# The sample's rows in the value products of heads 2 to 4: eight fp32 products on four column parts of the array

## The chip, the cores and the metric

The kernel runs on one core of one Trainium2 chip. The metric is the device time of one execution in microseconds (us), lower is better. Engines are named as in the profile: PE is TensorE (matrix products), PEld its weight load, DVE is VectorE, ACT is ScalarE, POOL is GpSimd, and SP is SyncE, whose queue issues nearly all DMAs here.

## What is computed

Two layers of a streaming encoder, for a prompt of 1024 tokens and, beside it, a sample of 32 tokens of another sequence with a carried state. Layer 0 mixes with an mLSTM (a matrix memory per head, four heads), layer 1 with attention in a band; each is followed by an MLP with squared ReLU. All is fp32. The part that matters here is the input of layer 0's mixer:

```python
def mlstm_mixer(u, ...):
    proj = u @ w_in                                   # u: tokens x 1024
    qk_pre = proj[..., :2 * QK_A]                     # 4 heads x 128, twice
    v = proj[..., 2 * QK_A:2 * QK_A + V_A]            # 4 heads x 256
    ...
    q, k = silu(causal_conv(qk_pre))                  # per head 128 wide
    # per chunk of tokens, per head: a matrix memory C (256 x 128)
    num = (q k^T * weights) v + a * (C q);  C = a_last * C + (w_s v)^T k
```

For each head, v is the product of all 1056 tokens (1024 of the prompt, then 32 of the sample) with 256 columns of `w_in`.

## The kernel before

**Number format of the products.** In the trace an fp32r product of 256 columns takes 0.12 us of PE, an fp32 product of 257 columns 0.44 us. To keep fp32 accuracy at the cheaper pace the kernel splits each operand into a high and a low fp32r part: ACT copies the raw value into the high part (L89) and DVE subtracts to get the low part (L90). A product is then three matmuls: high x high, high x low, low x high. `U` holds the modulated tokens already split (two parts, 8 chunks of 128 rows, 1056 tokens), and `wtile` loads 512 rows of a weight into a `raw` tile and splits it into a `w` tile.

**The value product.** `v_weight(h, half)` (L473) loads and splits one half (512 rows) of the 256 columns of head h. `v_chunk` (L483) does the three matmuls of one token tile and one chunk of rows; the tokens are the stationary operand (128 of them), the weights move (256 columns). There are NT = 9 token tiles: eight of the prompt and, as the ninth, the sample's 32 tokens, for which 128 columns of `U` are taken too (behind the last token lie 96 zero columns). A tile thus has 24 matmuls. `v_out` (L491) copies the result with ACT into a `vt` tile (tag "vt", nine buffers) and POOL writes 1.0 into two further columns.

`v_first` does head 1 (h = 0 in the code), three tiles at a time, with a chunk of each in turn, since its first tiles are produced only then; its eight extra columns are the gates. `v_proj` (L501) does heads 2 to 4 (h = 1 to 3), one tile after the other.

**The order of the work.** Per head h = 1 to 3 the program says `qk_proj(h)`, then `v_proj(h)`, then starts the recurrence `mlstm(h)`. `qk_proj` has 2 x 3 groups of 24 matmuls, then per half a convolution on DVE (L608 and L611, four passes) and a SiLU in three pieces of 353 columns (L613 to L618), each with a temporary of tag "tmp" (three buffers of 384 columns). The recurrence of head h - 1 is a generator: `flow.tick` lets it take one step (one chunk of 128 tokens) after each group or tile, so that its scores (L668, L669), sums (L686, L688) and updates (L690) come between the products of head h. Chunk 8, the last, is the sample; its start state comes in a `raw` tile (`cl`).

Outside the parts marked `manual_schedule` a planner sets the order on each engine and on each DMA queue from its own costs and from what waits for what. Buffers are shared by tag: PSUM tiles of tag "mm" (three buffers) serve the `qk`, `v` and `o` products; `raw` tiles (three buffers, of which one holds a sum of the conditioning, `ada_acc`, through this phase) serve all weights.

In the same phase the conditioning (`ada`) of the later parts is computed on DVE (L279 and the lines after it), a few operations per tick. `ada_mm` (L432) is the conditioning's first product, done at the start: fp32, with 32 stationary columns, on four column parts of the array side by side.

Of the kernel before, what the change touches and what calls it, by code (L numbers as in the profile page):

```python
# [8 lines left out]
F32 = mybir.dt.float32  # L9
F32R = mybir.dt.float32r  # L10
# [5 lines left out]
P = 128  # L16
D = 1024
KC = D // P
TP = 1024
TS = 32  # L20
T = TP + TS
NT = T // P + 1
# [53 lines left out]
def trunk_kernel(ctx: ExitStack, tc: tile.TileContext, a, o):  # L76
    nc = tc.nc
    flow = Flow()
    cp = ctx.enter_context(tc.tile_pool(name="const", bufs=1, reuse_waits="tile"))
# [4 lines left out]
    def raw_tile(shape, name):  # L84
        return ring.tile(shape, F32, tag="raw", name=name, bufs=3)

    def split(dst_h, dst_l, src, eng=None):

        nc.scalar.copy(dst_h, src)  # L89
        (eng or nc.vector).tensor_sub(dst_l, src, dst_h.bitcast(F32))  # L90

    def wtile(name, srcs, ncols=256, pool=None, eng=None, between=None):

        raw = raw_tile([P, 4, ncols], f"raw_{name}")
        for dst, src in srcs(raw):
            nc.sync.dma_start(dst, src)
        if pool is None:
            w = ring.tile([P, 2, 4, ncols], F32R, tag="wc", name=f"w_{name}", bufs=6)
        else:
            w = pool.tile([P, 2, 4, ncols], F32R, tag="h", name=f"w_{name}", bufs=5)  # L100
        if between:
            between()
        split(w[:, 0], w[:, 1], raw, eng)
        return w

    def wblock(name, src, r0, c0, eng=None):

        return wtile(name, lambda raw: [(raw, src[r0:r0 + 512, c0:c0 + 256].rearrange("(k p) c -> p k c", p=P))],
                     eng=eng)
# [19 lines left out]
    nc.vector.tensor_add(sel, ident[:, 0:32], ident[:, 32:64])  # L129
    for i in (64, 96):  # L130
        nc.vector.tensor_add(sel, sel, ident[:, i:i + 32])
    ones_d = cp.tile([P, P], F32R, name="ones_d")
    nc.vector.memset(ones_d.bitcast(F32), 1.0 / D)
    eps_ln = cp.tile([P, 1], F32, name="eps_ln")
    nc.vector.memset(eps_ln, LN_EPS)
    eps_hn = cp.tile([P, 1], F32, name="eps_hn")
# [36 lines left out]
    def mmt(name):  # L173
        return pa.tile([P, 512], F32, tag="mm", name=name, bufs=3)
# [191 lines left out]
    up_cm = tc.tile_pool(name="upool", bufs=1, side="right", reuse_waits="tile")  # L366
    upool = up_cm.__enter__()
    UF = KC * T
    U = upool.tile([P, 2 * UF + 96], F32R, name="U")
    nc.vector.memset(U[:, 2 * UF:].bitcast(F32), 0.0)  # L370

    def uap(hl, k, t0, n):
        off = hl * UF + k * T + t0
        return U[:, off:off + n]

# [11 lines left out]
    A = A_cm.__enter__()  # L387
# [82 lines left out]
    G = None  # L470
    cst = {}

    def v_weight(h, half):  # L473
        def srcs(raw):
            r0 = 512 * half
            r = [(raw[:, :, 0:256],
                  w_in[r0:r0 + 512, 1024 + h * 256:1024 + (h + 1) * 256].rearrange("(k p) c -> p k c", p=P))]
            if h == 0:
                r.append((raw[:, :, 256:264], w_in[r0:r0 + 512, 3072:3080].rearrange("(k p) c -> p k c", p=P)))
            return r  # L480
        return wtile(f"v{h}_{half}", srcs, 264 if h == 0 else 256)

    def v_chunk(ps, ws, t, k):  # L483
        w = ws[k // 4]
        n = w.shape[-1]
        uh, ul = uap(0, k, t * P, P), uap(1, k, t * P, P)
        nc.tensor.matmul(ps[:, :n], uh, w[:, 0, k % 4, :], start=(k == 0), stop=False)
        nc.tensor.matmul(ps[:, :n], uh, w[:, 1, k % 4, :], start=False, stop=False)
        nc.tensor.matmul(ps[:, :n], ul, w[:, 0, k % 4, :], start=False, stop=(k == KC - 1))

    def v_out(ps, h, t):  # L491
        m = P if t < NT - 1 else TS
        vt = A.tile([P, 258], F32, tag="vt", name=f"vt_{h}_{t}", bufs=9)
        nc.scalar.copy(vt[:m, :256], ps[:m, :256])
        nc.gpsimd.memset(vt[:m, 256:258], 1.0)
        if h == 0:
            nc.vector.tensor_copy(bass.AP(g64.tensor, g64[:m, t, 0:4].offset, [g64[:m].ap[0], [32, 2], [1, 4]]),
                                  ps[:m, 256:264].rearrange("p (a b) -> p a b", a=2))
        return vt

    def v_proj(h, after):  # L501
        ws = [v_weight(h, half) for half in range(2)]
        vts = []
        for t in range(NT):
            ps = mmt(f"v_{h}_{t}")
            for k in range(KC):
                v_chunk(ps, ws, t, k)
            vts.append(v_out(ps, h, t))
            after(t)
        return vts  # L510

    def v_first(ws, nxt):


        vts = []
        for bi, (t0, n) in enumerate(TBS):
            ts = range(t0 // P, (t0 + n + P - 1) // P)
            pss = {t: (mmt, nmt, mmt)[bi % 2 * (t % 2)](f"v_0_{t}") for t in ts}
            for k in range(KC):
                for t in ts:  # L520
                    v_chunk(pss[t], ws, t, k)
                nxt(bi, k)
            vts += [v_out(pss[t], 0, t) for t in ts]
        return vts
# [58 lines left out]
    def qk_proj(h, after):  # L583
        def srcs(r0):
            return lambda raw: [(raw[:, :, j * P:(j + 1) * P],
                                 w_in[r0:r0 + 512, j * 512 + h * P:j * 512 + (h + 1) * P].rearrange(
                                     "(k p) c -> p k c", p=P)) for j in range(2)]
        ws = [wtile(f"qk{h}_{i}", srcs(512 * i)) for i in range(2)]
        out = []
        for j in range(2):  # L590
# [181 lines left out]
    for k in range(2):  # L772
        ada_mm(k)
    vw = [v_weight(0, 0)]
    adaw += [ada_load(k) for k in (6, 7)]
    for k in range(2, 4):
# [5 lines left out]
    for k in range(6, 8):  # L782
        ada_mm(k)
    vw.append(v_weight(0, 1))
    x_load(*TBS[1])
    x_load(*TBS[2], wc_tile)
# [15 lines left out]
    vts = [v_first(vw, next_u)]  # L802
# [23 lines left out]
    for h in range(1, NH):  # L826
        unit = [0]

        def after_qk():
            unit[0] += 1  # L830
            if h > 1 or unit[0] >= 3:
                flow.tick()
        if h == 1:
            ml = flow.add(mlstm(0, *qk[0], vts[0]))
        qk.append(qk_proj(h, after_qk))
        vts.append(v_proj(h, tick))
        flow.finish(ml)
        ml = flow.add(mlstm(h, *qk[h], vts[h]))
# [35 lines left out]

    T_cm = tc.tile_pool(name="temps", bufs=1, reuse_waits="tile")
    T_ = T_cm.__enter__()

    def tmp_t(shape, name, dt=F32):
        return T_.tile(shape, dt, tag="t", name=name, bufs=5)

# [18 lines left out]
    def acc_dma(d, x, out=False):  # L899
        for i in range(0, KC, 4):  # L900
            p = [d[:, i:i + 4], x[:, i:i + 4]]
            nc.sync.dma_start(*(p if out else reversed(p)))
# [681 lines left out]
    mm, norm, _, out_proj, _, add_gated_at = make_layer(acc, bank, uap)  # L1584
# [38 lines left out]
    class L0:  # L1623
# [13 lines left out]
        def rows(k, n, hl):  # L1637
            return U[:, hl * UF + k * T:hl * UF + (k + n) * T].rearrange("p (k t) -> p k t", t=T)

# [30 lines left out]
        def after(blk):  # L1670
            t0, n = blk
            ti = TBS.index(blk)
            flow.finish(norms["ada"])
            norms[ti] = flow.add(norm(ti, 1, f"n01_{ti}", W01[ti], False, lambda ti: acc_dma(
                xsp[1][:, :, t0:t0 + n], acc[ti], True)), now=NOW)
# [11 lines left out]
    for gi, grp in enumerate(((0, 1, 2), (3,))):  # L1687
        ws = {pr: [wblock(f"q{pr}_{half}", wq, 512 * half, 256 * pr) for half in range(2)] for pr in grp}
        for ti, (t0, n) in enumerate(TBS):
# [9 lines left out]
            for fc in [f for pr in grp for f in (2 * pr, 2 * pr + 1)]:  # L1699
                g, r = fc // 2, 2 * (fc % 2)  # L1700
                gp, e = g // 2, g % 2
                ps = mm(f"q_{fc}_{t0}")
# [238 lines left out]
    for t in range(NT):  # L1941
# [4 lines left out]
        m = P if t < NT - 1 else TS  # L1946
# [220 lines left out]
```

## Time and profile before

| | |
|---|---|
| median of 3 runs | 2409.55 us (2406.93 to 2409.78) |
| profiled execution | 2412.41 us, span 2410.6 us |
| PE busy | 2342.7 us (97%), 17180 matmuls |
| PEld | 2250.4 us (93%) |
| DVE | 1939.0 us (80%) |
| ACT | 1206.0 us (50%) |
| POOL | 168.1 us (7%) |
| mean granted clock of TensorE | 0.995 |
| value products of heads 2 to 4 | first starts at 127.2 us, last at 307.2 us |

The span is the profiled part of an execution, and the time includes what lies around it. A matmul's busy time overlaps that of its neighbours, because matmuls are pipelined; the time that one takes from PE is the distance between two starts. In rows of instructions in order of time the columns are the start, the duration, engine, line, operation, the output and inputs, the part of the array (128*32 is 128 rows by 32 columns), the shape, and the count of instructions merged; in brackets stands the idle time ahead of it and what ended that. The phase of layer 0's mixer, in which the change lies, ends near 440 us.

### The profile page before, as it was taken

Reading aid. Unit: us, or ns where it says so; the run is one execution under the profiler, and the core shown is the slowest. Engines: PE = TensorE matmul, PEld = TensorE weight load, DVE = VectorE, ACT = ScalarE, POOL = GpSimd, SP = SyncE. Lnnn points to the kernel's source line nnn. Section 1 sums busy time; section 2 is a strip of 40 time slices with the busy share of each in tenths; the row PEclk is TensorE's granted clock in tenths of the full one; section 3 lists DMA queues with packets and bytes.
Section 4 is the critical chain, followed back from the end, with each engine's and each line's share of the span. In section 5 each row is a group of like instructions: output and inputs, shape, how many; then the busy total and the mean of one; then the engine's idle time right before and its main releaser. Section 6 shows DMA issues by size and latency. Waiting matters only on the chain. (4 is left out here: it accounts for less than half of the span.)

```text
span 2410.6 us, 44188 instructions
## 1 busy us (share of the span) xinstructions
PE 2342.7 (97%) x17180; PEld 2250.4 (93%) x17180; DVE 1939.0 (80%) x3903; ACT 1206.0 (50%) x2454; POOL 168.1 (7%) x320
## 2 busy tenths in 40 slices
PE   7999999999999999999999999999999999899997
PEld 4999999999999999999999987789999999899997
DVE  4888766778788789989888777756998889888778
ACT  4565557278666630101147467773776777222212
POOL 0111100000000000000000224420000000000003
PEclk9999999999999999999999999999999999999999
DMA  8343222526566896675512330051486779976642
GB/s 302 120 131 103 78 89 66 177 91 206 184 198 200 279 336 230 252 261 215 183 56 89 82 93 1 10 140 59 165 278 211 259 278 335 355 256 236 224 146 73
DMA packets 284277, 424.64 MB, mean 176 GB/s; under 512 B 15384, under 2 KB 205228, under 8 KB 278948
## 3 DMA queue, kind: packets, MB, share of 16 engines
q1 hardware_dynamic: 279860, 391.48, 48.3%
q10 hardware_dynamic: 4208, 30.35, 3.1%
q8 instruction: 135, 2.21, 0.4%
q14 instruction: 74, 0.61, 0.1%
HBM read 305.96 MB, written 118.17 MB: 176 GB/s over the span
## 5 line engine op out<-in xcount | busy, mean ns | idle before, releaser
L1082 DVE SCALAR_TENSOR_TENSOR ACX<-dn,ada,ACX 128x264 f32<-128x264 f32 (+6 forms) x664 | 281.8, 447 | 83.2 <-PE dn L1452 41.1
L1452 PE MATMUL dn<-fx,wf_d 128*128 128x264 f32 x2016 | 254.1, 285 | 6.8 <-DVE ACX L1082 3.5
L1452 PEld LDWEIGHTS dn<-fx,wf_d 128*128 128x128 f32 x2016 | 248.8, 188 | 9.0 <-DVE ACX L1082 3.0
L89 ACT CAST w_dn<-raw_dn 128x1024 fp32r<-128x1024 f32 x36 | 37.7, 1050 | 282.1 <-DVE aw L279 136.9
L118 PE MATMUL dn<-hs,w_dn 128*128 128x384 f32 (+2 forms) x512 | 161.2, 315 | 0.0
L119 PE MATMUL dn<-hs,w_dn 128*128 128x384 f32 (+2 forms) x512 | 161.0, 315 | 0.0
L120 PE MATMUL dn<-hs,w_dn 128*128 128x384 f32 (+2 forms) x512 | 156.4, 314 | 1.3 <-DVE w_dn L90 1.3
L1317 PE MATMUL up<-TF,wf_u 128*128 128x264 f32 x1056 | 143.2, 285 | 3.8 <-ACT H L1320 3.8
L1317 PE MATMUL up<-U,wf_u 128*128 128x264 f32 x1056 | 140.3, 285 | 1.7 <-ACT H L1320 1.2
L1317 PE MATMUL up<-u,wf_u 128*128 128x264 f32 x1056 | 139.7, 285 | 1.3 <-ACT wf_u L89 0.7
L279 DVE SCALAR_TENSOR_TENSOR aw<-radw,cs,aw 128x512 f32<-128x512 f32 x196 | 139.5, 743 | 1.1 <-DMA radw<-in_w_ada_dram 1.1
L1317 PEld LDWEIGHTS up<-TF,wf_u 128*128 128x128 f32 x1056 | 134.4, 189 | 4.8 <-ACT H L1320 4.6
L1317 PEld LDWEIGHTS up<-U,wf_u 128*128 128x128 f32 x1056 | 133.0, 188 | 3.0 <-ACT H L1320 1.6
L1317 PEld LDWEIGHTS up<-u,wf_u 128*128 128x128 f32 x1056 | 132.9, 188 | 1.9 <-ACT wf_u L89 0.9
L118 PE MATMUL dn<-U,w_dn 128*128 128x384 f32 (+2 forms) x416 | 129.4, 312 | 0.6 <-DVE ada L304 0.6
L119 PE MATMUL dn<-U,w_dn 128*128 128x384 f32 (+2 forms) x416 | 129.4, 312 | 0.0
L120 PE MATMUL dn<-U,w_dn 128*128 128x384 f32 (+2 forms) x416 | 125.9, 313 | 0.6 <-DVE w_dn L90 0.5
L1817 ACT ACTIVATE p<-p,mx 128x576 f32<-128x576 f32 (+9 forms) x132 | 86.6, 657 | 27.5 <-DVE mx L1814 25.2
L120 PEld LDWEIGHTS dn<-hs,w_dn 128*128 128x128 f32 x512 | 96.0, 188 | 2.0 <-DVE w_dn L90 1.8
L118 PEld LDWEIGHTS dn<-hs,w_dn 128*128 128x128 f32 x512 | 96.5, 189 | 0.1
L119 PEld LDWEIGHTS dn<-hs,w_dn 128*128 128x128 f32 x512 | 96.6, 189 | 0.0
L90 DVE TENSOR_TENSOR HL<-H,HL 128x1056 fp32r<-128x1056 f32 x64 | 80.3, 1254 | 20.0 <-ACT HL L89 19.9
(403 smaller groups left out, 7111.0 us busy)
## 6 DMA issues: line engine op xcount, KB each, us to landing
hpl<-HL SPq DMA_DIRECT2D x144, 264.0 KB
rdn_u<-in_w_up_dram SPq DMA_DIRECT2D x64, 512.0 KB
hd<-HL SPq DMA_DIRECT2D x28, 1056.0 KB
fx<-hd SPq DMA_DIRECT2D x50, 528.0 KB
radw<-in_w_ada_dram SPq DMA_DIRECT2D x24, 1024.0 KB
hd<-HM SPq DMA_DIRECT2D x28, 792.0 KB
raw_up<-in_w_up_dram SPq DMA_DIRECT2D x40, 512.0 KB
raw_dn<-in_w_down_dram SPq DMA_DIRECT2D x36, 512.0 KB
```

Source lines behind the costliest of these rows:

```text
L89: nc.scalar.copy(dst_h, src)
L90: (eng or nc.vector).tensor_sub(dst_l, src, dst_h.bitcast(F32))
L118: nc.tensor.matmul(ps, wh, mov(0, k), start=(k == 0), stop=False)
L119: nc.tensor.matmul(ps, wh, mov(1, k), start=False, stop=False)
L120: nc.tensor.matmul(ps, wl, mov(0, k), start=False, stop=(k == nk - 1))
L279: nc.vector.scalar_tensor_tensor(acc[cnd], raw[:, k], sc, acc[cnd], op0=ALU.mult, op1=ALU.add)
L1082: nc.vector.scalar_tensor_tensor(xs, ps[:, off + o:off + o + mm_], gate[:, fc, cnd:cnd + 1], xs, op0=ALU.mult, op1=ALU.add)
L1317: nc.tensor.matmul(p, self.ws[w][:, wl, k], moving(f, tp, xl, k), start=first and k + n_ == 0, stop=k == 3 and n_ == 2, skip_group_check=n ...
L1452: nc.tensor.matmul(p, ws[w][:, wl, k], t[:, s0, xl], start=first and k + n_ == 0, stop=k == kg - 1 and n_ == 2, skip_group_check=not first)
L1817: nc.scalar.activation(z, z, AF.Exp, bias=mx[:, 0:1], scale=-1.0, accum_out=mx[:, 1:2])
```

## The change

For heads 2 to 4 the sample leaves the row of tiles. `v_proj` now first adds the two parts of the sample's tokens back into plain fp32 (`us`, 128 x 8 x 32, in a buffer of tag "tmp"). While each half of the weight is loaded, and ahead of its split, `v_sample` multiplies four chunks of `us` with the raw fp32 weight, chunk k on column part k of the array, into the partitions 32k to 32k + 31 of one PSUM tile of tag "mm"; the second half adds to the first. `v_out` copies the first 32 partitions and adds the three others on DVE. Then one tick follows, and then the eight tiles of the prompt.

The sample's `vt` tile moves to a tag of its own ("vs", two buffers), and "vt" has eight buffers instead of nine. In head 1 the sample's tile now has 32 stationary columns instead of 128, so the 96 zero columns of `U` and their memset go. `ones_d`, a constant for the norms, moves from the pool of constants to the pool of temporaries that opens after this phase.

```diff
-            between()
+            between(raw)
         split(w[:, 0], w[:, 1], raw, eng)
...
-    ones_d = cp.tile([P, P], F32R, name="ones_d")
-    nc.vector.memset(ones_d.bitcast(F32), 1.0 / D)
...
-    U = upool.tile([P, 2 * UF + 96], F32R, name="U")
-    nc.vector.memset(U[:, 2 * UF:].bitcast(F32), 0.0)
+    U = upool.tile([P, 2 * UF], F32R, name="U")
...
-    def v_weight(h, half):
+    def v_weight(h, half, between=None):
...
-        return wtile(f"v{h}_{half}", srcs, 264 if h == 0 else 256)
+        return wtile(f"v{h}_{half}", srcs, 264 if h == 0 else 256, between=between)
...
     def v_chunk(ps, ws, t, k):
-        uh, ul = uap(0, k, t * P, P), uap(1, k, t * P, P)
+        m = P if t < NT - 1 else TS
+        uh, ul = uap(0, k, t * P, m), uap(1, k, t * P, m)
+        ps = ps[:m]
...
+    def v_sample(us, ps, half, raw):
+
+        for k in range(4):
+            nc.tensor.matmul(ps[32 * k:32 * k + 32, :256], us[:, 4 * half + k], raw[:, k], start=(half == 0),
+                             stop=(half == 1))
+
     def v_out(ps, h, t):
         m = P if t < NT - 1 else TS
-        vt = A.tile([P, 258], F32, tag="vt", name=f"vt_{h}_{t}", bufs=9)
+        vt = A.tile([P, 258], F32, tag="vt", name=f"vt_{h}_{t}", bufs=8) if m == P else \
+            A.tile([P, 258], F32, tag="vs", name=f"vt_{h}_{t}", bufs=2)
         nc.scalar.copy(vt[:m, :256], ps[:m, :256])
+        if m < P and h:
+            for q in range(1, 4):
+                nc.vector.tensor_add(vt[:m, :256], ps[32 * q:32 * q + m, :256], vt[:m, :256])
...
     def v_proj(h, after):
-        ws = [v_weight(h, half) for half in range(2)]
+        ps = mmt(f"v_{h}_s")
+        us = A.tile([P, 384], F32, tag="tmp", name=f"us_{h}", bufs=3)[:, :KC * TS].rearrange("p (k t) -> p k t", t=TS)
+        uv = U.rearrange("p (i k t) -> p i k t", i=2, t=T)[:, :, :, TP:].bitcast(F32)
+        nc.vector.tensor_add(us, uv[:, 0], uv[:, 1])
+        ws = [v_weight(h, half, lambda raw: v_sample(us, ps, half, raw)) for half in range(2)]
+        vs = v_out(ps, h, NT - 1)
+        after(NT - 1)
         vts = []
-        for t in range(NT):
+        for t in range(NT - 1):
             ps = mmt(f"v_{h}_{t}")
...
-        return vts
+        return vts + [vs]
...
     T_ = T_cm.__enter__()
+    ones_d = T_.tile([P, P], F32R, name="ones_d")
+    nc.vector.memset(ones_d.bitcast(F32), 1.0 / D)
```

## Prediction

> **What bounds the kernel now.** I read the page's first line, the busy time by stage, the groups of TensorE (PE) instructions in the stage, and then PE, ScalarE (ACT) and VectorE (DVE) in order of time around the value products of heads 2 to 4 (h = 1 to 3 in the code). The first rows are the page's span and three stages (length, then busy time of PE, PEld, DVE, ACT, POOL, the granted clock, DMA share, GB/s).
>
> ```profile
> span 2410.6 us, 44188 instructions
> ...
> 120.00:180.00 60.00, 58.68 (x407) 54.66 (x406) 52.19 (x128) 37.56 (x108) 10.52 (x30) 1.00 0.41 127
> 180.00:240.00 60.00, 58.57 (x416) 54.41 (x415) 51.67 (x124) 34.37 (x101) 8.65 (x30) 1.00 0.32 102
> 240.00:310.00 70.00, 69.50 (x483) 65.45 (x482) 46.60 (x116) 37.36 (x107) 8.47 (x29) 1.00 0.24 73
> ```
>
> PE works in 186.75 of these 190 us, so a microsecond of PE work or PE waiting here is a microsecond of the span. DVE is second, with 52 of 60 us in the first two stages. The executions shown have a median of 2409.55 us; the profiled one took 2412.41 us, 2.86 above it. My differences come from the profiled one and are set on the median.
>
> **What is removed.** One line of the value product in the stage (x count, busy, mean ns of one), and the pace of the last products of head 4, followed by a visit to narrow column parts (128*32):
>
> ```profile
> L487 PE MATMUL v<-w_v,U 128*128 128x256 f32 x216 | 63.4, 294 | 0.0
> ...
> 302.75 0.28 PE L487 MATMUL v<-w_v,U 128*128 128x256 f32 x1
> ...
> 307.18 0.28 PE L489 MATMUL v<-w_v,U 128*128 128x256 f32 x1
> 307.39 0.26 PE L301 MATMUL adas<-cx,sel 128*32 128x16 f32 x8
> 307.59 0.44 PE L118 MATMUL o<-U,w_o 128*128 128x384 f32 x1
> 307.87 0.33 PE L119 MATMUL o<-U,w_o 128*128 128x384 f32 x1
> 308.04 0.34 PE L120 MATMUL o<-U,w_o 128*128 128x384 f32 x1
> ```
>
> 216 is 3 heads x 9 tiles x 8 chunks, for each of three lines. From 302.75 to 307.18 lie 38 steps, so one takes 0.117 us. The sample's tile has 24 of them per head: 3 x 24 x 0.117 = 8.4 us of PE work go. The visit to the narrow parts shows a switch: 0.21 instead of 0.117 ahead of it, so 0.09 in, and 0.28 instead of 0.17 for the first 384-wide product behind it, so 0.11 out.
>
> **What is added on PE.** Per head eight fp32 products of 256 columns, four beside each other in each half. The nearest rows are the first conditioning product (fp32, 512 columns, on the same column parts), once with four parts and once with two, and two fp32 products of 257 columns on the whole array:
>
> ```profile
> 24.83 1.06 PE L435 MATMUL ada<-rada,cs 128*32 128x512 f32 x8
> ...
> 27.89 1.05 PE L435 MATMUL ada<-rada,cs 128*32 128x512 f32 x4 [1.99 <-DMA rada<-in_w_ada_dram]
> ...
> 119.68 0.60 PE L686 MATMUL num<-vt,sT 128*128 128x257 f32 x2
> 120.12 0.60 PE L690 MATMUL cu<-vt,kw 128*128 128x257 f32 x2
> ```
>
> An fp32 product leaves two records. Four parts (x8) take 1.06 us where two (x4) take 1.05: parts run beside each other. One product of 257 columns holds PE for 0.44 us, so a half costs 0.44, two halves in a row with one switch in and out 1.08, apart 1.28; if the four parts did not overlap, 2 x 1.76 + 0.2 = 3.7 per head. I take 1.1, since the 1.06 and 1.05 rows are of this very form: 3 x 1.1 = 3.3 us.
>
> The Trainium skill, page "TensorE: Matmul & The Clock Gate", section "Measured speedup vs the span model", measured three column parts at 2.38 times one, not 3 times. By that rate (an estimate from that page) four parts would give 3.17, a half 0.55 us, and the sum 0.7 us more. The rows above show no such loss.
>
> **Head 1 and the small edits.** Head 1 keeps its 24 products for the sample, now with 32 stationary columns. Its last block goes through the chunks with tiles 6, 7, 8 in turn, so PE enters and leaves a narrow part 8 times: 8 x 0.20 = 1.6 us, from 0 (if this counts as no switch) to 3.2 (twice the rows). PE is dense there and the gates wait for the result, so I count 1.6. On DVE come the sum into `us` and three sums of 32x256 per head, each below the 0.47 us that one of the two 353-column products at 210.38 takes (below): at most 1.9 us a head, of which `us` is ahead of PE (0.3 a head, 0.9 in all) and the three others lie in slack, because the sample's values are read only by the ninth step of the recurrence; without that slack they would cost up to 4.2. The two memsets that move or go are a tenth of a microsecond each at the start and off the path.
>
> **What the change puts in front of PE.** This decides. `us` takes a buffer of tag "tmp" (three buffers), behind the six SiLU pieces of `qk_proj(h)`; the PSUM tile of the sample takes a buffer of tag "mm" ahead of those of the eight prompt tiles. The planner gives out the buffers of one tag in the order of the program. A sign of it in the trace: GpSimd (POOL) idles and four buffers of tag "y" are free at the start, yet the margin memset of the first `qkp`, alone in its tag, runs at 1.55, and that of the second, which comes behind other "y" tiles in the program, only when one of these (`fr`) is done:
>
> ```profile
> 1.55 0.10 POOL L593 MEMSET qkp<- 128x3 f32 x1
> ...
> 91.86 0.14 POOL L593 MEMSET qkp<- 128x3 f32 x1 [3.96 <-DVE fr L558]
> ```
>
> So no prompt tile of v may begin before the sample's product begins, and that waits for `us`, which waits until the third SiLU piece of the key half has its buffer and the first piece has given one back. Head 3, and the ends for heads 2 and 4:
>
> ```profile
> 199.50 0.46 ACT L600 COPY qkp<-qk 128x256 f32<-128x256 f32 x2
> ...
> 200.81 0.47 PE L487 MATMUL v<-w_v,U 128*128 128x256 f32 x1
> ...
> 200.22 0.83 DVE L608 TENSOR_SCALAR y<-qkp,pt 128x1059 f32<-128x1059 f32 x1
> ...
> 206.79 0.89 ACT L459 ACTIVATE sl<-y 128x353 f32<-128x353 f32 x2
> ...
> 209.13 0.49 ACT L459 ACTIVATE sl<-y 128x353 f32<-128x353 f32 x1
> ...
> 210.38 0.94 DVE L617 SCALAR_TENSOR_TENSOR y<-y,sl 128x353 f32<-128x353 f32 x2
> ...
> 138.77 1.39 DVE L617 SCALAR_TENSOR_TENSOR y<-y,sl 128x353 f32<-128x353 f32 x3
> ...
> 280.31 0.96 DVE L617 SCALAR_TENSOR_TENSOR y<-y,sl 128x353 f32<-128x353 f32 x2
> ```
>
> In order: the last key columns leave PSUM at 199.5, four convolution passes run on DVE from 200.22, the first two SiLU pieces start on ACT at 206.79, the third at 209.13, and the first piece is read for the last time from 210.38 to 210.85. Then `us` can be written, and PE goes on at about 211.2. Today the v products begin at 200.81 and do not care. What they do in the three windows until then (v alone: PE, PEld, DVE, ACT; then the sum of all instructions):
>
> ```profile
> 127.20:139.50 12.30, 9.66 (x68) 8.65 (x68) 0.00 (x0) 0.54 (x2) 1.00 0.33 104
> 200.80:211.20 10.40, 9.22 (x67) 8.36 (x67) 0.00 (x0) 0.00 (x0) 1.00 0.42 126
> 270.00:281.10 11.10, 9.75 (x73) 9.02 (x74) 0.00 (x0) 0.37 (x1) 1.00 0.27 72
> ...
> sum 33.80, PE 33.49 PEld 31.93 DVE 33.57 ACT 23.52 POOL 6.80; mean PE 11.16 PEld 10.64 DVE 11.19 ACT 7.84 POOL 2.27
> ```
>
> 208 products x 0.117 = 24.3 us of PE work are pushed behind the wait, and PE has only the recurrence of the head before to do meanwhile. Could that run ahead? It needs DVE in every chunk, and DVE is busy in 33.57 of the 33.80 us, so hardly: between 0 and 2 chunks of 1.8 us a head (three products of 0.44, the scores and transposes the rest), of which I take 1 us a head, -3.0.
>
> **The clock.** Windows as above (the fourth number from the end is POOL, then the clock):
>
> ```profile
> 88.00:90.00 2.00, 1.59 (x10) 1.28 (x8) 2.00 (x2) 0.00 (x0) 0.00 (x0) 1.00 0.00 0
> 90.00:92.00 2.00, 0.00 (x0) 0.00 (x0) 2.00 (x5) 1.39 (x3) 0.14 (x2) 0.90 0.06 13
> 92.00:94.00 2.00, 1.99 (x12) 1.88 (x13) 1.51 (x3) 1.44 (x2) 0.74 (x1) 0.50 0.00 0
> ...
> 98.00:100.00 2.00, 2.00 (x15) 2.00 (x15) 2.00 (x3) 1.05 (x1) 0.29 (x1) 0.89 0.85 291
> ...
> 16.00:18.00 2.00, 0.47 (x3) 0.24 (x3) 0.00 (x0) 0.00 (x0) 0.00 (x0) 1.00 1.04 424
> ...
> 20.00:22.00 2.00, 2.00 (x7) 0.68 (x4) 0.34 (x1) 0.00 (x0) 0.00 (x0) 0.50 1.01 400
> ...
> 26.00:28.00 2.00, 0.11 (x2) 0.12 (x4) 1.42 (x2) 1.19 (x2) 0.00 (x0) 1.00 1.01 401
> 28.00:30.00 2.00, 1.77 (x8) 0.17 (x6) 1.10 (x1) 0.00 (x0) 0.00 (x0) 1.00 1.04 416
> ```
>
> 2.4 us of idle PE, from 89.6 to 92 (0.41 and 2.00 in the first two rows), were followed by a clock of 0.50 until about 98.2, that is 3.1 us lost; a quarter-busy PE at 16 to 18 by 0.50 at 20; a nearly idle one at 26 to 28 by nothing. The stalls leave PE a third busy for 10 us, so each costs 0 to 3.1; I take 1.5, the middle, since rows of both kinds lie equally near: 4.5.
>
> The Trainium skill, the same page, "What's actually happening", lets the clock fall only after an idle window of about 3.4 us. By that rule the scattered recurrence products would hold the clock up, and the sum would be 4.5 us less; the rows at 88 to 94, 0.50 after 2.4 us without PE work, say that less is enough.
>
> **Other queues.** The raw weights of v are now held until the sample's product has read them, so the loads behind them on the same buffers move from SP's present places to about 211 (head 3). A load takes until its split some 7 us, and the products of the next head begin at 239.35 and later:
>
> ```profile
> 200.26 0.37 SPq L96 DMA_DIRECT2D raw_v<-in_w_in_a_dram  x1
> ...
> 207.60 1.21 DVE L90 TENSOR_TENSOR w_v<-raw_v,w_v 128x1024 fp32r<-128x1024 f32 x1
> ...
> 239.35 0.34 PE L118 MATMUL qk<-U,w_qk 128*128 128x384 f32 x1
> ```
>
> Two such loads one after the other end near 226, so I cost this at nothing. Without that cover it would be up to 6 us a head.
>
> **Sum.** +24.3 - 3.0 + 0.9 - 8.4 + 3.3 + 1.6 + 4.5 = +23.2 us: 2435.6 against the profiled execution, 2432.8 against the median. Ends of the main case: 2428 (one chunk a head filled, -5.4, half the clock loss gone) to 2441 (nothing filled, the clock at 3.1 each). A difference below 0.2% (4.8 us) can't be told from none.
>
> **Rivals.** (a) No stall: a buffer for `us` is free in time, or the order inside a tag is not kept. For it: DVE is idle for 8 of 60 us in these stages; against it: the POOL rows. Then -8.4 + 3 x 1.28 + 1.6 = -3.0, 2406.6 us: not slower, and within what can be measured. It decides as soon as v products run before the first SiLU piece of the key half is done. (b) The stall is filled: PE idle lets the recurrence go two chunks a head ahead (-10.8 instead of -3.0) and keeps the clock up (-4.5): +10.9, 2420 us. For it: ACT is busy in only 23.5 of the 33.8 us; against it: DVE. (c) The loads held back come late for the next head: +6 a head, 2451 us. For it: few raw buffers; against it: 13 us of slack after two loads.
>
> **Chances.** Main case 0.62, (a) 0.14, (b) 0.18, (c) 0.06. The range from 2412 to 2442 leaves out (a) and (c), 0.20; the main case alone has 2428 to 2441. Slower by over 0.2%: main, (b), (c): 0.86. Of (a), 0.10 lies within 0.2% and 0.04 is faster (no switch cost in head 1 and a half at its least).
>
> **What would show it.** Right: in each of the three heads PE idle of 7 us or more that ends with `us` on DVE, ahead of the first v product; the 24 products of the sample replaced by 8 on 128*32; the clock below 1 behind a stall; 8 longer steps of 0.2 us in head 1's last block. Wrong: v products that start at the end of the key products, or a recurrence that fills the gap.

## Result and profile after

| | before | after |
|---|---|---|
| median of 5 runs each | 2409.55 us (2406.93 to 2411.81) | 2431.32 us (2429.3 to 2433.66) |
| the profiled execution | 2412.41 us | 2429.3 us |
| end of the last v product of head 4 | 307.2 us | 328.6 us |
| end of the last op_a product | 515.4 us | 536.7 us |

The ratio after to before is 1.0092, 95% interval 1.0077 to 1.0106: the kernel became slower by 21.8 us in the medians. The forecast was 2432.8, in a range from 2412 to 2442.

The first rows of the page of after and its busy time by stage (length, then PE, PEld, DVE, ACT, POOL, the granted clock, DMA share, GB/s) answer to the first rows of the prediction:

```profile
span 2427.5 us, 44155 instructions
...
120.00:180.00 60.00, 53.35 (x354) 46.55 (x353) 50.81 (x124) 34.30 (x100) 9.03 (x26) 0.91 0.37 114
180.00:240.00 60.00, 53.44 (x335) 46.14 (x334) 47.40 (x112) 31.78 (x92) 12.09 (x27) 0.91 0.30 99
240.00:310.00 70.00, 63.67 (x432) 58.52 (x431) 55.82 (x131) 35.94 (x102) 11.42 (x27) 0.95 0.31 95
```

PE was busy in 186.75 of these 190 us and is now in 170.46, at a clock below 1. To compare like with like, cut each trace from the end of head 1's v products to the end of head 4's, before first, then after:

```profile
69.60:307.40 237.80, 231.98 (x1561) 218.48 (x1560) 192.71 (x423) 138.30 (x373) 38.49 (x104) 0.99 0.32 99
```

```profile
69.30:328.60 259.30, 236.41 (x1544) 214.13 (x1542) 211.97 (x458) 139.22 (x373) 44.48 (x103) 0.94 0.33 103
```

The stretch is 21.5 us longer: 17.1 of it is added idle time of PE (5.8 to 22.9), 4.4 is added busy time, although PE has 72 fp32r products less and only 24 fp32 ones more. So there are two losses, waiting and slower work. Head 3 in order of time shows both (start, duration, engine, line; in brackets the idle time before and what ended it):

```profile
206.32 0.30 PE L120 MATMUL qk<-U,w_qk 128*128 128x288 f32 x1
...
207.26 0.46 ACT L615 COPY qkp<-qk 128x256 f32<-128x256 f32 x2
...
213.12 0.70 PE L705 MATMUL cu<-vt,kw 128*128 128x257 f32 x2 [0.91 <-ACT sm L724]
...
216.37 0.95 DVE L459 SCALAR_TENSOR_TENSOR sl<-y,sl 128x353 f32<-128x353 f32 x2
...
217.70 0.52 DVE L632 SCALAR_TENSOR_TENSOR y<-y,sl 128x353 f32<-128x353 f32 x1
...
219.20 1.23 PE L705 MATMUL cu<-vt,kw 128*128 128x257 f32 x2 [3.21 <-ACT sm L724]
...
219.67 0.42 DVE L514 TENSOR_TENSOR us<-U 128x256 f32<-128x256 f32 x1
...
221.22 1.94 PE L493 MATMUL v_s<-raw_v,us 128*32 128x256 f32 x16
...
223.08 0.58 PE L486 MATMUL v<-w_v,U 128*128 128x256 f32 x1
```

The key products end at 206.6. The first SiLU piece is read for the last time from 217.70, `us` follows at 219.67, the sample's product at 221.22, the first prompt product of v at 223.08. Between 206.6 and 221.2 PE has only the recurrence. The sample's product takes 1.94 us and the first v product 0.58, about twice the 1.07 and 0.28 that the same shapes take at full clock (in a run below): the clock had fallen.

```profile
212.00:214.00 2.00, 0.91 (x3) 0.30 (x2) 2.00 (x5) 0.54 (x3) 0.47 (x2) 1.00 0.46 179
214.00:216.00 2.00, 1.41 (x4) 0.68 (x4) 1.51 (x6) 2.00 (x6) 0.21 (x2) 0.82 0.00 0
216.00:218.00 2.00, 0.00 (x0) 0.00 (x0) 1.97 (x6) 1.80 (x5) 0.24 (x1) 0.50 0.29 103
...
222.00:224.00 2.00, 2.00 (x16) 1.12 (x9) 1.01 (x3) 0.36 (x1) 0.00 (x0) 0.50 0.24 70
224.00:226.00 2.00, 2.00 (x13) 2.00 (x13) 1.94 (x7) 0.00 (x0) 0.00 (x0) 0.62 0.73 195
```

The fourth number from the end is POOL, then comes the clock: below 1 from about 215 to 225, in which dense v products already ran.

### The profile page after: what moved, and what is told of

It is laid out like the page before. It is cut to its first block, busy times and chain, and to the rows that moved or that the text cites. A ratio compares the mean times of both kernels' runs of the same rounds, so it can differ in the third digit from the quotient of the medians.

```text
span 2427.5 us, 44155 instructions
## 1 busy us (share of the span) xinstructions
PE 2343.9 (97%) x17156; PEld 2244.4 (92%) x17156; DVE 1947.0 (80%) x3914; ACT 1206.2 (50%) x2454; POOL 174.1 (7%) x320
```

## Experiments

The theory: a prompt tile of v can't begin until the sample's PSUM tile, ahead of it in tag mm, has been given its buffer, and that happens with the first product into it, which waits for `us`, which waits for a tmp buffer behind the SiLU pieces. The rivals: the fp32 product itself (its switches, the raw weights it holds), the new order of the tiles, or the late product whatever the tags. All ratios are to the kernel before, run beside each experiment on its own chip; its median was 2407.6 to 2408.4 us there, so times of different experiments can lie about 1 us apart from that alone.

**The wait taken away, the product kept.**

```
-  us = A.tile([P, 384], F32, tag="tmp", ...)      (per head)
+  us = G[:, 7, 0:KC * TS]                         (written once, ahead of the loop over heads)
```

> The sum `us` is written once, into a part of G that nothing needs before head 4's recurrence, so it no longer asks for a tmp buffer; the fp32 product stays as it is, ahead of the prompt tiles. Theory (the wait for the tmp buffer is the loss): no stall ahead of v in heads 2 to 4, the clock stays at 1.00 there, and the time is that of before less 8.4 for the 72 products plus 3.3 for the new ones: 2404.5 us, 2401 to 2408. Rival (the fp32 product itself, its switches, the held raw weights or the clock they bring are the loss): 2428 to 2432, as the changed kernel.

Measured: 2407.7 us, ratio 0.9996 (0.9987 to 1.0004). The stall is gone: the sample's product of head 2 starts at 125.0, right behind the key products, instead of 137.4, and v ends at 302.3 instead of 328.6. The rival falls for the fp32 product and its switches, which are all still there. The raw weights are given back early here; that holding them until `us` is there is no loss either is shown by the runs with another PSUM tag and with one useless product, which hold them that long. The forecast of 2404.5 was missed by 3 us; the run with both cures comes back to that.

**The wait kept, the product taken away.**

```
+  us (fp32r, tag "tmp") = copy of U's upper half
+  24 products v_s<-w_v,us / w_v,U, 32 stationary columns, ahead of the prompt tiles
-  8 fp32 products from the raw weights, and the three sums on DVE behind them
```

> The sample's tile is again 24 fp32r products with the split weights, but first in the program, and its stationary operand is a copy of U's upper half that takes a tmp buffer behind the SiLU pieces, as `us` did: the wait without the fp32 product. Theory: the stall is as in the changed kernel, and 3 x (24 x 0.117 - 1.1) = 5.1 us of product come on top: 2436 us, 2432 to 2440. Rival (the fp32 product and the held raw weights are the loss): 2409 to 2413.

Measured: 2435.3 us, ratio 1.0118 (1.0101 to 1.0134). The same stretch as above, and the longest waits of PE in this kernel (us in total, times, longest):

```profile
70.00:331.20 261.20, 239.61 (x1569) 218.98 (x1567) 209.63 (x454) 139.50 (x373) 36.80 (x103) 0.94 0.33 103
```

```profile
PE cu L707 <- ACT sm L726: 8.4, 4, 4.4
PE num L703 <- DVE ct L710: 6.4, 5, 2.0
```

The wait alone gives the loss: 21.6 us idle (261.20 less 239.61), the clock 0.94, without one fp32 product of the change.

**The order alone.** As the run before, with the products reading U directly instead of the copy.

> As the run with the fp32r product behind the tmp wait, but the products read U directly: the sample's tile comes first in the program and waits for nothing. Theory: the order alone costs nothing, 2409.5 us, 2407 to 2412, no stall. Rival (taking the sample first is what disturbs the order on PE): 2425 to 2435.

Measured: 2408.81 us, ratio 1.0001 (0.9992 to 1.0010). To take the sample first costs nothing as long as it waits for nothing. In this kernel the sample's tiles have 32 stationary columns in all four heads, so those cost nothing either.

```profile
70.00:305.60 235.60, 228.97 (x1560) 214.64 (x1558) 193.09 (x423) 138.55 (x373) 40.76 (x103) 1.00 0.33 100
```

**The late `us` kept, the PSUM tag changed.**

```
-  ps = mmt(f"v_{h}_s")
+  ps = nmt(f"v_{h}_s")
```

> The changed kernel with `us` still in tmp and late, but with the sample's PSUM tile taken from the tag of the recurrence (nm) instead of mm. Theory (the mm order is what makes the prompt tiles wait for a late `us`): the v products start at the end of the key products, the sample's eight come some 10 us later in their midst, and the time is 2404.5 to 2408 us. Rival (the wait for `us` or the late product holds up PE whatever its PSUM tag, in the order of the program): 2428 to 2432.

Measured: 2404.35 us, ratio 0.9986 (0.9978 to 0.9995). `us` is written at 136.7 to 276.8, as late as ever, but the v products no longer care. Head 4 in order of time, then the stretch:

```profile
277.36 0.28 PE L488 MATMUL v<-w_v,U 128*128 128x256 f32 x1
277.57 1.07 PE L493 MATMUL v_s<-raw_v,us 128*32 128x256 f32 x16
278.57 0.70 PE L701 MATMUL num<-vt,sT 128*128 128x257 f32 x2
```

```profile
70.80:302.60 231.80, 225.16 (x1536) 208.37 (x1534) 198.43 (x435) 138.66 (x373) 39.07 (x103) 1.00 0.33 102
```

So of the two tags it is mm that carries the wait on to the prompt tiles. One line turns a loss of 0.9% into a gain of 0.14%, and this version beats both kernels.

**One useless product.**

```
   nc.vector.tensor_add(us, uv[:, 0], uv[:, 1])
+  nc.tensor.matmul(ps[:, :256], uap(0, 0, 0, P), uap(0, 0, 0, 256), start=True, stop=True)
```

> The changed kernel with one useless fp32r product per head into the sample's own PSUM tile (the sample's products overwrite it). `us` stays in tmp and as late as it was, the sample's tile stays first in mm; but the tile is begun before `us` is there. It computes nothing that is used. Theory (a prompt tile waits until the sample's tile has been given its buffer, which happens with the first product into it): the v products start at the end of the key products, 27 us come back for 3 x 0.12 us of added work: 2404 to 2408 us. Rival (PE keeps the order of the program, or the late product itself holds it up): 2428 to 2432.

Measured: 2405.31 us, ratio 0.9984 (0.9975 to 0.9993). The tile is begun at 125.57, v goes on at 127.32, and the sample's product follows 9 us later:

```profile
125.57 0.37 PE L518 MATMUL v_s<-U 128*128 128x256 f32 x1
...
127.32 0.36 PE L486 MATMUL v<-w_v,U 128*128 128x256 f32 x1
...
136.71 1.07 PE L493 MATMUL v_s<-raw_v,us 128*32 128x256 f32 x16
```

This is the sharpest test: only the first product into the tile is moved, and 25 to 26 us come back (25 against the changed kernel on the same chip, below). The rivals predicted no gain.

**Both cures.** `us` early and the sample's tile in nm.

> Both cures at once: `us` written once into the free part of G, and the sample's PSUM tile from nm. Theory: nothing holds the prompt tiles and nothing holds the sample; the 5.1 us of the exchanged products remain: 2403 to 2406 us. Rival (what the early `us` alone gave back, 0.7 instead of 5 us, is a cost of the early sample): 2406 to 2409.

Measured: 2407.37 us, ratio 0.9999 (0.9990 to 1.0008). As with the early `us` alone, some 3 us short of the two runs with a late `us`. In the traces the end of v does not tell them apart (302.3 and 302.7 with the early `us`, 302.5 and 300.8 with the late); the profiled executions differ in stages behind it. Why an early sample product costs 3 us was not settled.

**The sample last.** The sample's tile, `us` and the eight products moved behind the eight prompt tiles, so that both raw weights are held until then.

> The changed kernel with the sample's part (its PSUM tile in mm, `us` in tmp, the eight fp32 products) behind the eight prompt tiles in the program. `us` is then never late, but both raw weights of v are held until the end of the v products, some 24 us longer than in the kernel before. Theory (only the wait ahead of the prompt tiles costs; held raw weights are covered): 2404.5 us, 2402 to 2409, no stall. Rival (held raw weights delay the next head's loads): up to 6 us a head, 2415 to 2424, with PE waiting for w_qk at the start of heads 3 and 4.

Measured: 2427.0 us, ratio 1.0083 (1.0069 to 1.0096). No wait for `us`, and yet nearly the whole loss. The theory's part of this expectation fell, and the rival named the wrong tile: `w_qk` is in time. The waits of PE, and the first of them in order of time:

```profile
PE clp L678 <- DMA cl<-in_state_C_dram: 12.9, 3, 5.2
```

```profile
161.46 0.25 PE L299 MATMUL adas<-cx,sel 128*32 128x16 f32 x8
165.27 0.66 PE L678 MATMUL clp<-ident,cl 128*128 128x128 f32 x2 [3.56 <-DMA cl<-in_state_C_dram]
```

The load of the state for the recurrence's ninth step (`cl`, in `scores`) takes a raw buffer as well, behind the weights in the program. It was held up in each of the three heads, PE stood still for 12.9 us in all and ran at half clock behind it (the row at 165.27 has 0.66 us for two products of 128 columns). The stage of `o` is 127.0 us long here, against 112.6 in the changed kernel. Held raw buffers are a price of their own; the change escapes it because it gives them back at the first products of v, not the last.

**Filling the stall.** 72 useless products per head into the sample's own tile.

> The changed kernel with 72 useless fp32r products (U by U, 256 columns) per head into the sample's own PSUM tile ahead of the sample's products (which overwrite it): they depend on no `us`, so they run inside the stall. They compute nothing that is used. Theory (the clock is a term of its own: behind the stalls the changed kernel ran at 0.50 for some 4, 3 and 4 us): the clock stays at 1.00, the stalls stay as long, and 7.5 us come back less up to 3 for the recurrence that the useless products push back: 2424 to 2427 us. Rival (the low clock costs nothing here, because PE waits for DVE anyway): 2431 to 2434.

Measured: 2429.23 us, ratio 1.0093 (1.0080 to 1.0107). Neither theory's reading stands, because the run did not do what it was made for: as the run with one useless product shows, a product into the sample's tile opens it, so there was no wait left. PE ran the 216 useless products instead:

```profile
L518 PE MATMUL v_s<-U x216: 279/279/468, 126.8 to 294.0; 128*128 128x256 f32 x108
```

```profile
69.30:328.10 258.80, 252.17 (x1750) 236.21 (x1749) 199.63 (x434) 138.81 (x373) 39.07 (x103) 0.98 0.29 91
```

At 0.117 us each they are 25.3 us, and the run is 24.9 above the one with the tile in nm; its idle time is 6.6, as there. It says nothing of the clock.

**Useless products elsewhere.** 36 per head into three tiles of the tag tp, so that the wait stays.

> The changed kernel with 36 useless fp32r products per head (U by U, 256 columns, 4.2 us) into PSUM tiles of the tag tp, three of 12, so that the sample's tile is not begun by them: the wait for `us` stays and the prompt tiles stay behind it, but PE has more to do in the stall. They compute nothing that is used. Theory (half clock behind a stall is a loss of its own, some 3 us a head, and a busier PE keeps the clock up): stalls as long as before, 6 to 9 us back: 2422 to 2426 us. Rival (the clock falls all the same, or costs nothing): 2430 to 2434.

Measured: 2433.6 us, ratio 1.0106 (1.0090 to 1.0122). In heads 2 and 3 the clock held, in head 4 it fell for two windows; head 3 first, then head 4:

```profile
214.00:216.00 2.00, 1.13 (x4) 0.68 (x4) 1.91 (x7) 1.74 (x6) 0.37 (x2) 1.00 0.00 0
216.00:218.00 2.00, 0.96 (x4) 0.59 (x4) 2.00 (x7) 1.84 (x9) 0.00 (x0) 1.00 0.71 228
...
291.00:293.00 2.00, 1.37 (x16) 0.60 (x16) 2.00 (x9) 2.00 (x8) 0.00 (x0) 0.58 1.02 351
```

The stage followed the theory in part: v ends at 324.0 instead of 328.6 and op_a at 531.9 instead of 536.7, 4.8 us sooner. The time did not: behind op_a the profiled execution took 1887.6 us to the last of PE's work on the output (`yt`), the changed kernel 1879.3. The code of those stages is the same in all thirteen profiled executions of this document, and they take from 1879.3 to 1887.6 us there: these two are the ends of that scatter. Why the median is nevertheless not below that of the changed kernel stays open.

**Fewer of them, beside the changed kernel once more.** 24 per head in the tag tp, and the changed kernel unaltered on the same chip.

> As the run with 36 useless products per head in tp, with 24 (two tiles of 12, 2.8 us). They compute nothing that is used. Theory (the low clock is a loss of its own): the stage up to the last product of op_a ends 4 to 8 us sooner than in the changed kernel, as with 36, and since less useless work is done than the 17 us that PE idles, the whole time follows: 2424 to 2428 us. Rival (what PE does in the stall changes nothing, or the stages behind take back what it gives): 2430 to 2434.

> The changed kernel once more, beside the run with 24 useless products on the same chip, so that the two are set against each other: 2429 to 2433 us, the end of op_a some 536.7 us after the start by every theory.

Measured: 2429.55 us (ratio 1.0083, 1.0071 to 1.0096) with the 24 products, 2430.12 (1.0087, 1.0073 to 1.0100) without. The clock fell in all three heads with 24 too: in head 3 later than in the unaltered kernel (from 219.6 instead of 214.6 us on), in heads 2 and 4 sooner (134.3 instead of 136.1, 291.3 instead of 293.1), and for 17 us in all instead of 24. op_a ends at 534.8, and at 535.4 in the changed kernel. No difference that can be measured. So the low clock is seen in the traces and accounted for below, but no run gave its price back in the whole time.

## Why the prediction was right, and which of its terms were not

The main mechanism is shown: the wait alone makes the loss, each of three ways to break it (an early `us`, another PSUM tag, one product that opens the tile) removes it, and the order and the fp32 product do not make it. What makes `us` late was not split further: it takes a tmp buffer, as the prediction says, but in head 3 DVE writes it 1.5 us after the first SiLU piece is read for the last time (217.70 + 0.52 to 219.67), with other work in between, so its place in the order of DVE has a part in it. Rival (a), no stall, is refuted by the stalls. Rival (b), the stall filled by the recurrence, is not what happened, but it had a point (below). Rival (c), late loads, did not occur in this kernel.

Two of the signs named ahead came: 8 products instead of 24, and a clock below 1 at each stall. Two did not: the longer steps in head 1 (below), and an idle time of PE of 7 us or more that ends with `us`. The three windows from about the end of the key products to the sample's product, then the longest waits of PE in the changed kernel:

```profile
125.40:137.40 12.00, 6.23 (x28) 3.94 (x29) 11.38 (x29) 8.04 (x28) 1.91 (x7) 0.83 0.28 88
206.00:221.20 15.20, 9.25 (x45) 5.93 (x45) 13.58 (x29) 9.43 (x30) 3.64 (x11) 0.81 0.41 141
283.00:296.30 13.30, 6.97 (x41) 4.49 (x39) 11.86 (x24) 9.37 (x31) 3.85 (x11) 0.91 0.30 96
```

```profile
PE cu L705 <- ACT sm L724: 9.5, 4, 4.4
PE num L701 <- DVE ct L708: 6.1, 5, 1.7
PE v_s L493 <- DVE us L514: 1.9, 2, 1.7
```

PE idles 5.8, 6.0 and 6.3 us in them, and only 1.9 us of its waits end with `us`. The v products are held by `us`, but the recurrence runs meanwhile, and PE waits for the steps of that.

The sum of the prediction against the stretch of 237.8 and 259.3 us:

| term | predicted, us | measured, us | from |
|---|---|---|---|
| v pushed behind the wait, less recurrence run ahead, plus `us` (24.3 - 3.0 + 0.9) | +22.2 | +17.1 | idle 5.8 to 22.9 |
| products removed and added (-8.4 + 3.3) | -5.1 | -3.8 | PE busy 228.97 (order alone) to 225.16 (tile in nm) |
| narrow tile in head 1 | +1.6 | 0 | rows below |
| clock behind the stalls | +4.5 | +9.5 | PE busy 236.41 to 225.16, less 1.7 |
| the dip at 92 to 98, in both kernels | 0 | -1.3 | 3.0 before, 1.7 after |
| sum | +23.2 | +21.5 | |

Four terms were off and nearly cancelled: the mechanism was right, but that the total is so near is luck.

*The recurrence run ahead.* I allowed 1 us of it a head, because DVE was full. 24.3 less 17.1 leaves 7.2 (8.1 with `us`), 2.4 to 2.7 a head, nearer to the 3.6 of rival (b). This is what an estimate and a measured idle time leave between them, not a direct measurement of the recurrence. DVE is busy in 36.8 of the 40.5 us of the three windows above, less full than the 33.57 of 33.80 that I went by. The wait itself had nearly the predicted length: from the last key columns to the sample's product it is 11.6, 14.0 and 11.8 us (125.78 to 137.36, 207.26 to 221.22, 284.54 to 296.30), where I had counted 11.7 (199.5 to 211.2). The 2.3 us more in head 3 do not come from the convolution, which is not slower in the stall (6.6 us from 207.26 to the first SiLU piece at 213.90, 7.3 before): DVE has other work ahead of `us` at 219.67, and PE then does two products of the recurrence at half clock, from 219.20 on, ahead of the sample's product.

*The sample's product* has nearly the predicted size: in the run with the tile in nm its two halves hold PE for 1.00 us (277.57 to 278.57), 0.50 each, where I took 0.44. What else makes the exchange worth 3.8 instead of 5.1 us was not traced. The estimate from the Trainium skill, page "TensorE: Matmul & The Clock Gate", section "Measured speedup vs the span model", was 0.55 a half; the measured 0.50 lies between it and the rows.

*Head 1.* The order alone, with narrow tiles in all heads, costs nothing, and the rows of the changed kernel show no switch:

```profile
64.69 0.28 PE L487 MATMUL v<-w_v,U 128*128 128x264 f32 x1
64.81 0.28 PE L486 MATMUL v<-w_v,U 128*32 128x264 f32 x1
...
68.07 0.28 PE L488 MATMUL v<-w_v,U 128*32 128x264 f32 x1
68.19 0.28 PE L486 MATMUL v<-w_v,U 128*128 128x264 f32 x1
```

The steps are 0.12 into the narrow part and out of it. The row I had priced it by was a visit of fp32 products, and a visit of fp32 products on the narrow part again shows 0.21 ahead of it (277.36 to 277.57 above). What costs 0.1 is then not the narrow part by itself.

*The clock.* I took 1.5 us a head from bounds of 0 to 3.1; the busy time gives 3.2. The changed kernel and the one with the tile in nm run the same products, so the difference of their busy time is the slower clock: 11.25 us, of which the dip at 92 to 96 is 1.7 (clock 0.60 and 0.54):

```profile
92.00:94.00 2.00, 2.00 (x13) 1.94 (x13) 1.92 (x3) 1.18 (x2) 0.47 (x1) 0.60 0.03 4
94.00:96.00 2.00, 2.00 (x10) 2.00 (x9) 2.00 (x6) 0.48 (x1) 0.00 (x0) 0.54 0.15 30
```

The granted clock agrees: it is 0.50 from 133.37 to 143.61, 215.29 to 225.53 and 293.80 to 300.63, PE is busy in 20.9 us of these, and half of that is 10.5. Of this 7.4 us lie behind the start of the sample's product (3.1, 2.2 and 2.2 a head), within the bounds but well above their middle; the other 3.0 lie inside the stalls, where the prediction has no such term and where a faster PE might have waited instead.

*The loads at nothing.* Right for this kernel, but the reason looked at the wrong load: the run with the sample last shows that, when the raw weights are held longer, PE waits for `cl`, which the prediction did not name.

*Against the median.* In the profiled pair the spans differ by 16.9, not 21.5. The difference lies in a later stage: from the end of op_a to the first product of dn, before took 351.3 us, after 347.4, and all others shown between 347.2 and 349.5. There PE waited longer in the profiled execution of before (the longest waits of PE from 505 to 890, before, then after):

```profile
PE up L1317 <- ACT H L1320: 4.8, 6, 1.5
```

```profile
PE up L1334 <- ACT H L1337: 2.0, 3, 0.9
```

The medians, 21.8 apart, agree with the edited stage.

## What to carry to other kernels

Where buffers of one tag are given out in the order of the program, a tile that waits for something late holds up every later tile of its tag, whether or not these depend on it. Before moving a tile to the front, ask what its first instruction waits for, and if that is late, take its buffer from another tag (here one word, from 1.0092 to 0.9986). A cost that is read off one neighbouring row (the narrow visit) should be checked for what else differs in that row, and of two kernels with the same work the difference in busy time comes near the price of the clock (here 9.5 us for the three stalls, where the clock itself gives 10.5).

## What was not expected of the hardware

The clock fell without a long gap. Head 2 of the changed kernel, PE in order of time:

```profile
129.23 0.70 PE L701 MATMUL num<-vt,sT 128*128 128x257 f32 x2 [1.56 <-DVE ct L708]
129.77 0.60 PE L703 MATMUL num<-ct,qc 128*128 128x257 f32 x2
131.32 0.70 PE L705 MATMUL cu<-vt,kw 128*128 128x257 f32 x2 [0.96 <-ACT sm L724]
133.53 1.23 PE L701 MATMUL num<-vt,sT 128*128 128x257 f32 x2 [1.51 <-DVE ct L708]
```

No gap is over 1.6 us, and the product at 133.53 already takes nearly twice the time of the one at 129.23. In the second profile of the same kernel the clock was still 1.00 there until 136. And 2.4 us of idle PE may cost nothing: the kernel with the order alone idles as long as before did (all of 90 to 92 and 0.39 us behind it) and keeps the full clock where before fell to 0.50 for 6.8 us (91.6 to 98.4):

```profile
90.00:92.00 2.00, 0.00 (x0) 0.00 (x0) 2.00 (x3) 1.05 (x2) 0.00 (x0) 1.00 0.06 13
92.00:94.00 2.00, 1.61 (x14) 1.56 (x15) 1.91 (x5) 1.79 (x3) 0.88 (x2) 1.00 0.00 0
```

That dip is worth 3.0 us of the profiled execution of before (231.98 less 228.97) and is not a property of its code. The changed kernel shows this too: with 2.4 us of idle PE there in both of its profiles, the clock falls in the first (0.60 and 0.54 from 92 to 96, above) and stays at 1.00 in the second. How long the clock stays low is less free. Cut finely, every spell of 0.50 in the thirteen traces, but the one at the very end of the program, is 3.4, 6.8, 10.2 or 13.7 us long; so 3.4 us of it cost a busy PE 1.7 us, and each stall of the changed kernel brought two or three times that length.

The Trainium skill, page "TensorE: Matmul & The Clock Gate", section "What's actually happening", says that the clock drops after an idle window of about 3.4 us and that the window runs freely, so that the same kernel can meet it at different points. The varying point agrees with these traces; the idle window of 3.4 us does not, since scattered products with gaps of 1.6 us did not hold the clock up.
